# Values before queries in a cross-attention, and two products that walk pass by pass

## The chip, the cores and the metric

The kernel runs on one core of a Trainium2 chip. Its time is the device time of one execution in microseconds (us). Several runs are taken, and their median is the figure that is compared. One further execution is recorded by the hardware profiler, and all views of the profile come from that one.

The engines of a core are called PE (TensorE, matrix products; PEld is its loading of weights), DVE (VectorE), ACT (ScalarE), POOL (GpSimd) and SP (SyncE, which here only issues transfers). Each runs its own queue of instructions in order, and semaphores hold an instruction back until what it needs is there.

## The reference

One layer of a streaming encoder on 512 tokens of width 1024, with 256 memory tokens. What matters here is its middle and the beginning of its last part:

```python
mixed = jnp.sum(gates * proj, axis=2) @ w_out[l]
x = x + _rms_norm(mixed, norm_mix_post[l])

hx = _rms_norm(x, norm_x_pre[l])
m = _rms_norm(mem, norm_mem[l])
xq = (hx @ w_xq[l])                              # 4 heads of 128
xk, xv = jnp.split(m @ w_xkv[l], 2, axis=-1)
sx = einsum('bqhd,bkhd->bhqk', xq, xk) * (X_HEAD_DIM ** -0.5)
px = softmax(sx, axis=-1)
ox = einsum('bhqk,bkhd->bqhd', px, xv).reshape(B, S, X_W) @ w_xo[l]
x = x + _rms_norm(ox, norm_x_post[l])

hf = _rms_norm(x, norm_ffn_pre[l])
u = _dwconv_causal(hf @ w_up[l], ffn_dw[l]) + ffn_dw_b[l]
u_g, u_v = jnp.split(u, 2, axis=-1)
x = x + _rms_norm((silu(u_g) * u_v) @ w_down[l], norm_ffn_post[l])
```

Keys and values (`xk`, `xv`) depend on the memory alone, not on `x`. The queries depend on `hx`, which is only there when the mixers' output projection has been normed.

## The kernel before

**Products in three passes.** All products are kept near fp32 precision by splitting each operand into a high part (fp32r) and a low part (the rest). `mm3` (L185) then issues three matmuls for one product: high weight with high activation, high with low, low with high. The high part of a split is a copy on ACT, the low part a subtraction on DVE (`split`, L106, with its instructions at L109 and L110).

**Weights.** `run_blocks` (L151) draws a list of jobs. A job is one block of weights, 512 KB, and a body that uses it. The block is loaded by SP into one of two raw buffers (`wr`, L123), copied by ACT into one of four high buffers (`wh`, L138), and subtracted by DVE into one of four low buffers (`wl`, L139). Two blocks are fetched ahead. A raw buffer is free for its next load when the low part of the block in it has been made, and a high buffer when the last matmul of the block in it is through.

**The order of the jobs** (`all_jobs`, L1268) is: the mixers, the output projection `mix_out_jobs`, the keys `kx_jobs` (4 blocks), the queries `xq_jobs` (4 blocks), the values `vx_jobs` (4 blocks), the output of the cross-attention `cross_out_jobs` (4 blocks of `w_xo`), the up projection `up_jobs` (44 blocks), the down projection (22 blocks).

- `kx_jobs` (L962) and `xq_jobs` (L1105) use blocks of 128 columns over the full contraction of 1024 (8 pieces of 128). A block gives 24 matmuls of 256 columns, for 256 memory tokens or for half the queries. `xq_jobs` projects the first half of the tokens (tiles 0 and 1) for each head as its block comes, after `drain("n0")`; with the fourth block it drains `"n1"` and projects the second half for all four heads, `part(g, 1)`, out of the four blocks it holds.
- `vx_jobs` (L970) uses blocks of 256 rows of the contraction and all 512 columns. Each gives 12 matmuls of 512 columns, into two PSUM banks that stay open over the four blocks; after the last, both are split into `vxh` and `vxl`.
- `cross_out_jobs` (L1152) holds its four blocks, and then for each half computes `cross_values` (softmax weights times values, into `ox`) and the output product of two tiles.
- `up_jobs` (L1188) computes its first four blocks for the first half of the tokens as the blocks come. With the fourth it drains the last norms and computes the second half of all four (`held`). From the fifth block on the full 512 columns are done at once.

**Work in the background.** `Background` (L44) holds tasks that are written as generators: the softmax of one head and half of the queries (`cross_task`, L1075: scores, exponentials, then transposes into `pth` and `ptl`), and the norm of one tile (`norm_task`, L1000: the residual sum `res`, the squares, the normed tile `nt`, then eight transposes on PE, whose result is split into `hth` and `htl`, the turned activations). A tick lets tasks advance when the foreground has issued enough matmuls; a drain finishes them.

**The final order** on each engine is settled by the framework's scheduler, which moves instructions within what the data allow. The orders of the two built programs can be laid side by side.

**`channel_major`** (L191) is the loop that the change gives a second form of. It goes through the pieces `k` of the contraction and issues the three matmuls of a piece together, so the second matmul already needs the low part of the activations.

Of the kernel before, what the change touches and what calls it, by code (L numbers as in the profile page):

```python
# [25 lines left out]
S = 512  # L26
# [54 lines left out]
def hybrid_layer(ctx: ExitStack, tc: tile.TileContext, a: dict, out: bass.AP):  # L81
# [8 lines left out]
    def bank(tag="mm"):  # L90
        return psum.tile([P, 512], F32, tag=tag, name=f"ps_{tag}", bufs=4 if tag == "mm" else 2)
# [14 lines left out]
    def split(ps, hi, lo, scale=None):  # L106

        if scale is None:
            A.copy(hi, ps)  # L109
            V.tensor_tensor(lo, ps, hi.bitcast(F32), ALU.subtract)  # L110
        else:
            A.activation(hi, ps, AF.Copy if isinstance(scale, float) else AF.Identity, scale=scale)
            V.scalar_tensor_tensor(lo, ps, scale, hi.bitcast(F32), ALU.mult, ALU.subtract)
# [31 lines left out]
    def cols(w, c0, n=P, k0=0, nk=NK):  # L145

        return w[k0 * P:(k0 + nk) * P, c0:c0 + n].rearrange("(k p) c -> p k c", p=P), [P, nk, n]
# [29 lines left out]
    def matmul(ps, lhs, rhs, start, stop):  # L177
        PE.matmul(ps, lhs, rhs, start=start, stop=stop)  # L178
        bg.clock += max(int(math.prod(rhs.shape[1:])), 256) * 0.00042
# [5 lines left out]
    def mm3(ps, w_hi, w_lo, x_hi, x_lo, first, last):  # L185

        matmul(ps, w_hi, x_hi, first, False)
        matmul(ps, w_hi, x_lo, False, False)
        matmul(ps, w_lo, x_hi, False, last)

    def channel_major(ps, w, act, sl=slice(0, S)):  # L191

        hi, lo = w
        nk = hi.shape[1]
        for k in range(nk):
            mm3(ps[:, sl], hi[:, k, :], lo[:, k, :], act[0][:, k, sl], act[1][:, k, sl], k == 0, k == nk - 1)
            if k == 3 < nk - 1:
                bg.tick()

    def rstd_of(pool, parts, n=1):  # L200

        m = pool.tile([P, n], F32, tag="st_m", name="st_m", bufs=4)
        r = pool.tile([P, n], F32, tag="st_r", name="st_r", bufs=4)
        if len(parts) == 2:
            G.tensor_scalar(m, parts[0], parts[1], EPS, ALU.add, ALU.add)  # L205
        else:
            G.tensor_scalar(m, parts[0], EPS, None, ALU.add)
        G.tensor_tensor(r, m, nhalf[:, :n], ALU.pow)  # L208
        return r
# [80 lines left out]
    for i, plan in enumerate(plans):  # L290
        r_t = m1p.tile([P, P], F32, tag="fbias" if i == 2 else "ck", name=f"rows{i}", bufs=2)
        n = 0
# [601 lines left out]
    def then(f):  # L894

        return None, None, f
# [27 lines left out]
    ns = SimpleNamespace()  # L924
# [37 lines left out]
    def kx_jobs():  # L962
        for h in range(4):
            def body(hi, lo, h=h):
                ps = bank()
                channel_major(ps, (hi, lo), ns.mt, slice(0, MEM))
                split(ps[:, :MEM], ns.kx[0][:, h], ns.kx[1][:, h])
            yield *cols(w_xkv, h * P), body

    def vx_jobs():  # L970
        st = {}
        for kb in range(4):
            def body(hi, lo, kb=kb):
                if kb == 0:
                    st["ps"] = [bank() for _ in range(2)]
                for t in range(2):
                    sl = slice(t * P, (t + 1) * P)
                    for k in range(2):
                        kk = kb * 2 + k
                        mm3(st["ps"][t], ns.mt[0][:, kk, sl], ns.mt[1][:, kk, sl], hi[:, k], lo[:, k],  # L980
                            kk == 0, kk == NK - 1)
                    if kb == 3:
                        split(st["ps"][t], ns.vx[0][:, t], ns.vx[1][:, t])
            yield *cols(w_xkv, BR, BR, kb * 2, 2), body
# [90 lines left out]
    def cross_task(h, half):  # L1075

        ps = bank("sc")
        for i in range(2):
            q = slice((2 * half + i) * P, (2 * half + i + 1) * P)
            mm3(ps[:, i * MEM:(i + 1) * MEM], ns.xq[0][:, h, q], ns.xq[1][:, h, q], ns.kx[0][:, h],  # L1080
                ns.kx[1][:, h], True, True)
        p2 = ps.rearrange("p (i k) -> p i k", i=2)
        st = ns.xp.tile([P, 8], F32, tag="st8", name="st8", bufs=4)
        e = ns.xp.tile([P, 2, MEM], F32, tag="xe", name="xe", bufs=5)
        V.tensor_reduce(st[:, 0:2], p2, AX.X, ALU.max)
        V.tensor_scalar(st[:, 2:4], st[:, 0:2], -xscale, None, ALU.mult)
        for i in range(2):
            A.activation(e[:, i], p2[:, i], AF.Exp, bias=st[:, 2 + i:3 + i], scale=xscale,
                         accum_out=st[:, 4 + i:5 + i])
        V.reciprocal(st[:, 6:8], st[:, 4:6])  # L1090
        for i in range(2):
            V.tensor_scalar(e[:, i], e[:, i], st[:, 6 + i:7 + i], None, ALU.mult)
        yield 1.4, 6.0
        while half == 1 and (h, 0) in ns.pt:
            yield 0.0, 0.5
        ps = bank("tr")
        for kt in range(2):
            for i in range(2):
                transpose(ps[:, (2 * kt + i) * P:(2 * kt + i + 1) * P], e[:, i, kt * P:(kt + 1) * P])
        pt = tuple(ns.xp.tile([P, 2, 2 * P], F32R, tag=n, name=n, bufs=4) for n in ("pth", "ptl"))  # L1100
        split(ps.rearrange("p (k c) -> p k c", k=2), pt[0], pt[1])
        ns.pt[h, half] = pt
        yield 0.6, 0.0

    def xq_jobs():  # L1105
        held = []
        for h in range(4):
            def body(hi, lo, h=h):
                held.append((hi, lo))

                def part(h, half):
                    sl = slice(half * 256, (half + 1) * 256)
                    ps = bank()
                    channel_major(ps, held[h], ns.hx, sl)
                    split(ps[:, sl], ns.xq[0][:, h, sl], ns.xq[1][:, h, sl])
                    bg.add(cross_task(h, half), f"x{half}")
                    bg.tick()

                if h == 0:
                    bg.drain("n0")  # L1120
                part(h, 0)
                if h == 3:
                    bg.drain("n1")
                    for g in range(4):
                        part(g, 1)
            yield *cols(w_xq, h * P), body
# [61 lines left out]
    def up_jobs():  # L1188
        st, held = {}, []

        def done(j, i, ps):
            if i == 0:
                st[j] = ns.fp.tile([P, 2, S], F32, tag="c", name="c", bufs=2)
            c, ch = st[j], i * NF + j
            A.activation(c[:, i], ps, AF.Identity, bias=pc("fb", ch), scale=pc("fdw2", ch))  # L1195
            taps(c[:, i], ps, lambda k: pc("fdw01", k * 44 + ch), 3)
            if i == 1:
                th = ns.fp.tile([P, S], F32, tag="th", name="th")
                A.activation(th, c[:, 0], AF.Tanh, scale=0.5)
                V.scalar_tensor_tensor(th, th, 1.0, c[:, 0], ALU.add, ALU.mult)  # L1200
                V.scalar_tensor_tensor(c[:, 1], th, 0.5, c[:, 1], ALU.mult, ALU.mult)  # L1201
                split(c[:, 1], ns.act[0][:, j], ns.act[1][:, j])


        for n in range(2 * NF):
            def body(hi, lo, n=n):
                j, i = divmod(n, 2)
                if n > 3:
                    ps = bank()
                    channel_major(ps, (hi, lo), ns.hf)  # L1210
                    done(j, i, ps)
                    return
                if n == 0:
                    bg.drain("n0")
                ps = bank("mm" if n % 2 else "sc")
                channel_major(ps, (hi, lo), ns.hf, slice(0, S // 2))
                held.append((j, i, ps, (hi, lo)))
                if n == 3:
                    open_ffn()
                    for j, i, ps, w in held:  # L1220
                        channel_major(ps, w, ns.hf, slice(S // 2, S))
                        done(j, i, ps)
            yield *cols(w_up, n % 2 * DFF + n // 2 * P), body

# [43 lines left out]
    def all_jobs():  # L1268
        yield from mixer_jobs()
        yield from last_branch_jobs()  # L1270
        yield then(open_mix_out)
        yield from mix_out_jobs()
        yield then(lambda: bg.drain("mem"))
        yield from kx_jobs()
        yield then(open_cross)
        yield from xq_jobs()
        yield from vx_jobs()
        yield then(open_cross_out)
        yield from cross_out_jobs()
        yield from up_jobs()  # L1280
        yield from down_jobs()

    run_blocks(all_jobs())
    close(ns.fp_)
    close(ns.res_)
# [27 lines left out]
```

## Time and profile before

| | |
|---|---|
| median of 3 runs | 1109.14 us (1108.85 to 1110.48) |
| the profiled execution, its own time | 1108.61 us |
| its span, first to last instruction | 1106.8 us |
| PE busy | 1091.0 us, 99% of the span |
| DVE, ACT, POOL busy | 693.9, 464.9, 97.9 us |
| mean granted clock of PE | 0.998 |

Times in the views are counted from the start of the span. PE's matmuls overlap by a little, so the distance from one start to the next tells its pace better than the length of one. In a view of instructions in order of time, the columns are start and length in us, engine, line, operation, result and inputs by the program's names, size and number; a bracket at the end gives the idle time before it and the instruction that ended the idle time. The keys begin at about 641 us, the queries at 655, the values at about 686, the up projection at 731.

### The profile page before, as it was taken

How to read it: one execution, taken by the hardware profiler on the slowest of the kernel's cores; microseconds unless marked ns; L12 is line 12 of the kernel's file. 1: busy time of each engine (PE TensorE's matmuls, PEld its weight loads, DVE VectorE, ACT ScalarE, POOL GpSimd, SP SyncE). 2: the span in 40 equal slices, each digit the busy share in tenths (PEclk: the TensorE clock that was granted, in tenths of full speed). 3: DMA queues.
4: the chain of work that ended last, by engine and by line, in shares of the span. 5: the costliest groups of instructions: out<-in, count | busy, mean ns of one | idle time of the engine just before them, and what ended most of it. 6: DMA issues, size and time to landing. Idle time of an engine off the chain costs nothing.

```text
span 1106.8 us, 14168 instructions
## 1 busy us (share of the span) xinstructions
PE 1091.0 (99%) x5445; PEld 913.1 (82%) x5445; DVE 693.9 (63%) x1128; ACT 464.9 (42%) x783; POOL 97.9 (9%) x186
## 2 busy tenths in 40 slices
PE   8999999999999999999999999999999999999997
PEld 7888888887878988888888899788888888888886
DVE  5899985457665367857464477677666666642224
ACT  5322222467564255554443365455444444431111
POOL 3000001000101013323010110120000000000001
PEclk9999999999999999999999999999999999999999
DMA  6433432332212243233262253233333333322222
GB/s 197 115 95 94 102 94 81 92 96 58 77 58 78 77 120 104 82 96 107 65 209 96 76 174 115 73 96 115 95 95 95 96 95 95 96 96 95 95 76 76
DMA packets 145849, 109.29 MB, mean 99 GB/s; under 512 B 3648, under 2 KB 133293, under 8 KB 145782
## 3 DMA queue, kind: packets, MB, share of 16 engines
q1 hardware_dynamic: 143221, 99.85, 29.9%
q0 software_dynamic: 2560, 8.54, 2.8%
q8 instruction: 43, 0.70, 0.3%
q14 instruction: 25, 0.20, 0.1%
HBM read 106.27 MB, written 2.11 MB: 98 GB/s over the span
## 4 chain that ended last, share of the span: by engine, by line
PE 94%; DVE 2%; DMA 1%; issue 1%; ACT 1%; POOL 0%; POOLq 0%; DVEq 0%; SPq 0%; ACTq 0%
PE ps_mm L178 80%; PE ps_sc L178 7%; PE ps_tr L182 3%; PE ps_tr L178 3%; PE ps_mm L359 1%; DVE wl L139 1%; DMA wr<-in_w_xo 1%; DMA wr<-in_w_xkv 0%; ACT wh L138 0%; DMA xs<-in_x 0%; POOL st_r L208 0%; DVE e L671 0%; PE ps_tr L343 0%; PE ps_mm L343 0%; ACT hth L109 0%
## 5 line engine op out<-in xcount | busy, mean ns | idle before, releaser
L139 DVE TENSOR_TENSOR wl<-wr,wh 128x1024 fp32r<-128x1024 f32 (+1 forms) x180 | 221.4, 1231 | 221.6 <-ACT wh L138 220.9
L178 PE MATMUL ps_mm<-htl,wh 128*128 128x512 f32 (+1 forms) x944 | 359.9, 381 | 0.0
L178 PE MATMUL ps_mm<-hth,wh 128*128 128x512 f32 (+1 forms) x944 | 359.8, 381 | 0.0
L178 PE MATMUL ps_mm<-hth,wl 128*128 128x512 f32 (+1 forms) x944 | 358.7, 380 | 0.0
L138 ACT CAST wh<-wr 128x1024 fp32r<-128x1024 f32 (+1 forms) x180 | 188.6, 1050 | 349.1 <-PE ps_mm L178 223.0
L178 PEld LDWEIGHTS ps_mm<-hth,wl 128*128 128x128 f32 x944 | 177.4, 188 | 34.5
L178 PEld LDWEIGHTS ps_mm<-hth,wh 128*128 128x128 f32 x944 | 177.6, 188 | 33.9
L178 PEld LDWEIGHTS ps_mm<-htl,wh 128*128 128x128 f32 x944 | 177.6, 188 | 33.0
L507 DVE SCALAR_TENSOR_TENSOR y<-y,par,y 128x499 f32<-128x499 f32 (+28 forms) x120 | 82.7, 729 | 0.2
L178 PE MATMUL ps_mm<-y,wh 128*128 128x512 f32 x256 | 81.2, 395 | 0.0
L441 DVE SCALAR_TENSOR_TENSOR c<-ps_mm,par,c 128x510 f32<-128x510 f32 x84 | 62.6, 746 | 1.4
L178 PEld LDWEIGHTS ps_mm<-y,wh 128*128 128x128 f32 x256 | 47.4, 188 | 10.1
L178 PE MATMUL ps_mm<-y,wl 128*128 128x512 f32 x128 | 50.6, 395 | 0.0
L205 POOL TENSOR_SCALAR st_m<-pm,pm 128x1 f32<-128x1 f32 x12 | 4.6, 387 | 480.6 <-ACT junk L1254 357.0
L109 ACT CAST acth<-c 128x512 fp32r<-128x512 f32 x22 | 13.7, 621 | 55.2 <-DVE c L1201 55.2
L109 ACT CAST pth<-ps_tr 128x512 fp32r<-128x512 f32 (+3 forms) x56 | 23.7, 451 | 27.8 <-PE ps_tr L182 24.9
L178 PE MATMUL ps_mm<-wh,actl 128*128 128x512 f32 x88 | 34.7, 394 | 0.0
L178 PE MATMUL ps_mm<-wl,acth 128*128 128x512 f32 x88 | 34.6, 393 | 0.0
L178 PE MATMUL ps_mm<-wh,acth 128*128 128x512 f32 x88 | 34.4, 394 | 0.0
L110 DVE TENSOR_TENSOR ptl<-ps_tr,pth 128x512 fp32r<-128x512 f32 (+3 forms) x56 | 27.8, 512 | 9.5 <-ACT pth L109 9.1
L1195 ACT ACTIVATE c<-ps_mm,par 128x512 f32<-128x512 f32 x42 | 32.5, 773 | 0.0
L830 POOL TENSOR_SCALAR fbias<-ck,cq 128x128 f32<-128x128 f32 (+3 forms) x32 | 25.5, 805 | 70.6 <-DVE st L836 66.9
(294 smaller groups left out, 1620.3 us busy)
## 6 DMA issues: line engine op xcount, KB each, us to landing
wr<-in_w_up SPq DMA_DIRECT2D x44, 512.0 KB
wr<-in_w_in SPq DMA_DIRECT2D x38, 512.0 KB
wr<-in_w_gate SPq DMA_DIRECT2D x32, 512.0 KB
wr<-in_w_down SPq DMA_DIRECT2D x22, 512.0 KB
wr<-in_w_branch SPq DMA_DIRECT2D x16, 512.0 KB
wr<-in_w_out SPq DMA_DIRECT2D x8, 512.0 KB
wr<-in_w_xkv SPq DMA_DIRECT2D x8, 512.0 KB
wr<-in_w_in SPq DMA_DIRECT2D x4, 520.0 KB
```

The lines of the kernel that those rows point to most:

```text
L109: A.copy(hi, ps)
L110: V.tensor_tensor(lo, ps, hi.bitcast(F32), ALU.subtract)
L138: order(A.copy(hi[:, :n], raw[:, :n]))
L139: low.tensor_tensor(lo[:, :n], raw[:, :n], hi[:, :n].bitcast(F32), ALU.subtract)
L178: PE.matmul(ps, lhs, rhs, start=start, stop=stop)
L182: PE.transpose(ps, x, ident[:n, :n])
L205: G.tensor_scalar(m, parts[0], parts[1], EPS, ALU.add, ALU.add)
L359: keep(PE.matmul(banks[c][:, :S // 2], w[p == 1][:, k, c * P:(c + 1) * P], ht[p == 2][:, i * 4 + k, :S // 2], start=(i, p, k) == (0, 0, 0) ...
L441: V.scalar_tensor_tensor(dst[:, s:], src[:, :S - s], w(k), dst[:, s:], ALU.mult, ALU.add)
L507: V.scalar_tensor_tensor(dst[:, s:], src[:, :S - s], pc("conv_dw", k * 4 + j), dst[:, s:], ALU.mult, ALU.add)
L830: G.tensor_scalar(bias[:, :w], ck[j][:, :w], -1.0, cq[:, qt, head:head + 1], ALU.mult, ALU.add)
L1195: A.activation(c[:, i], ps, AF.Identity, bias=pc("fb", ch), scale=pc("fdw2", ch))
```

## The change

The values are projected directly behind the keys, ahead of the queries. And a new loop, `by_pass`, takes the place of `channel_major` in three places: for head 0 of the queries, in both halves of the tokens, for the first block of the up projection in the first half of the tokens, and for the same block in the second half. It goes over the contraction in two halves of four pieces, and within a half does four matmuls of high with high, four of low weights with high activations, four of high weights with low activations. It does not call `bg.tick()` in the middle, which `channel_major` does. Everything else is as it was.

```diff
+    def by_pass(ps, w, act, sl):
+
+        hi, lo = w
+        nk = hi.shape[1]
+        for h in range(2):
+            ks = range(h * nk // 2, (h + 1) * nk // 2)
+            for i, (w_p, x_p) in enumerate(((hi, act[0]), (lo, act[0]), (hi, act[1]))):
+                for k in ks:
+                    matmul(ps[:, sl], w_p[:, k, :], x_p[:, k, sl], i == k == 0, i == 2 and k == nk - 1)
...
                     ps = bank()
-                    channel_major(ps, held[h], ns.hx, sl)
+                    (channel_major if h else by_pass)(ps, held[h], ns.hx, sl)
...
                 ps = bank("mm" if n % 2 else "sc")
-                channel_major(ps, (hi, lo), ns.hf, slice(0, S // 2))
+                (channel_major if n else by_pass)(ps, (hi, lo), ns.hf, slice(0, S // 2))
...
                     for j, i, ps, w in held:
-                        channel_major(ps, w, ns.hf, slice(S // 2, S))
+                        (channel_major if i or j else by_pass)(ps, w, ns.hf, slice(S // 2, S))
                         done(j, i, ps)
...
         yield from kx_jobs()
+        yield from vx_jobs()
         yield then(open_cross)
         yield from xq_jobs()
-        yield from vx_jobs()
         yield then(open_cross_out)
         yield from cross_out_jobs()
```

## Prediction

> **What bounds the kernel now.** I read the page first: the busy times, the chain that ended last, the granted clock. TensorE (PE) is busy for 99% of the span, holds 94% of the chain, and runs at its full clock in all 40 slices.
>
> ```profile
> PE 1091.0 (99%) x5445; PEld 913.1 (82%) x5445; DVE 693.9 (63%) x1128; ACT 464.9 (42%) x783; POOL 97.9 (9%) x186
> ...
> PEclk9999999999999999999999999999999999999999
> ...
> PE 94%; DVE 2%; DMA 1%; issue 1%; ACT 1%; POOL 0%; POOLq 0%; DVEq 0%; SPq 0%; ACTq 0%
> ```
>
> The change removes no matmul, so it can act only through moments in which PE stands still. The instruction orders of the two built programs say where to look: they agree on every engine up to the first query product (655.33 in the profile before) and again from the fifth up-projection block (about 755). The table by stretches and the list of what PE waited for cover that stretch and the one ahead of it.
>
> ```profile
> 640.00:655.00 15.00, 14.26 (x117) 13.80 (x116) 14.19 (x17) 8.48 (x15) 3.54 (x8) 1.00 0.58 176
> 685.00:700.00 15.00, 14.54 (x78) 12.22 (x76) 9.11 (x15) 7.33 (x12) 0.00 (x0) 1.00 0.49 167
> 700.00:710.00 10.00, 8.90 (x47) 7.21 (x48) 5.75 (x15) 4.36 (x13) 0.00 (x0) 1.00 0.18 54
> 730.00:740.00 10.00, 9.67 (x75) 8.99 (x74) 9.11 (x11) 6.17 (x12) 3.19 (x4) 1.00 0.50 144
> 740.00:750.00 10.00, 9.76 (x82) 9.33 (x81) 3.17 (x4) 1.49 (x3) 1.35 (x3) 1.00 0.21 71
> ...
> PE ps_mm L178 <- DVE vxl L110: 0.8, 1, 0.8
> PE ps_tr L182 <- DVE xe L1092: 0.7, 1, 0.7
> PE ps_mm L178 <- ACT wh L138: 0.7, 1, 0.7
> PE ps_sc L178 <- ACT hth L109: 0.2, 1, 0.2
> PE ps_sc L178 <- DVE htl L110: 0.2, 1, 0.2
> ```
>
> First number behind the comma: PE's busy time in the stretch. The 0.7 us behind `wh` lies in the keys (640 to 655) and stays. The others add to two pieces: the end of the values (`vxl`, `xe`, near 700) and the start of the up projection (`htl`, `hth`, near 732 and 745). So at most some 3 us of 1108.61 are to be had.
>
> **What goes: the wait at the values.** Today the values are the last thing projected before they are used, and the last half of the queries' softmax has just begun. These are the starts of PE's instructions there.
>
> ```profile
> 699.26 0.28 PE L178 MATMUL ps_mm<-ptl,vxh 128*128 128x256 f32 x1
> 700.35 0.38 PE L178 MATMUL ps_mm<-pth,vxl 128*128 128x256 f32 x1 [0.81 <-DVE vxl L110]
> ...
> 702.00 0.28 PE L178 MATMUL ps_mm<-pth,vxl 128*128 128x256 f32 x1
> 703.02 0.72 PE L182 MATMUL ps_tr<-ident,xe 128*128 128x128 f32 x4 [0.74 <-DVE xe L1092]
> 703.73 0.50 PE L178 MATMUL ps_mm<-wh,oxh 128*128 128x512 f32 x1
> ...
> 569.50 48.85 PE ps_mm L178 x211
> 557.26 0.87 PE ps_tr L182 x8
> 655.37 4.65 PE ps_mm L178 x39
> ```
>
> The last three rows, from the chain in order of time, give PE's undisturbed pace: 48.85/211 = 0.232 us for a 512-column matmul, 4.65/39 = 0.119 for a 256-column one, 0.109 for a transpose. Against them the starts lose 1.09 - 0.12 = 0.97, 1.02 - 0.12 = 0.90 and 0.71 - 0.44 = 0.27 us: **2.1 us**. In the new order `vx` is done before the first query product, and the softmax of the first half runs beside the 96 matmuls (11.4 us) of the queries' second half, so these waits go. What is late next: with no values in between, the first softmax transposes of the second half stand behind two further score blocks and among the output products; I find cover for each.
>
> **What goes: the start of the up projection.** Here PE waits for the transposed second tile, high part (ACT) and low part (DVE).
>
> ```profile
> 731.43 0.28 PE L178 MATMUL ps_mm<-hth,wh 128*128 128x256 f32 x1
> 731.85 0.39 PE L178 MATMUL ps_sc<-hth,wh 128*128 128x256 f32 x1
> 732.44 0.38 PE L178 MATMUL ps_sc<-htl,wh 128*128 128x256 f32 x1 [0.20 <-DVE htl L110]
> ...
> 746.01 0.28 PE L178 MATMUL ps_mm<-hth,wh 128*128 128x256 f32 x1
> 746.27 0.39 PE L178 MATMUL ps_sc<-htl,wh 128*128 128x256 f32 x1
> ```
>
> Lost over 0.12 per step: 0.30 + 0.47 = 0.77 us, and 0.14 in the second half. By passes, eight matmuls that need only the high part (4 of `wh`, 4 of `wl`, 0.95 us) stand ahead of the first that needs `htl`. That covers 0.47 and 0.14. The 0.30 is a wait of block 2's first product, which the built order moves behind block 1. Gone: **0.9 us**. `by_pass` itself issues the same 24 matmuls per block at the same pace: no cost. At the queries it removes nothing, since nothing waits there today.
>
> **What comes: twelve weight blocks in a row.** The values' 4 blocks (12 matmuls of 512 columns, 2.78 us each) now stand between the keys' 4 and the first-half queries' 4 (24 of 256, 2.86 us). SP's load of block n+2 waits until DVE has made the low part of block n (two raw buffers), so a buffer's cycle is landing + cast + low part against 5.6 us of PE. Today the queries' second halves, which need no weights, part the eight from the next eight. The four loads of values move past the four of queries on SP's queue; POOL's order is unchanged.
>
> ```profile
> 653.32 1.22 DVE L139 TENSOR_TENSOR wl<-wr,wh 128x1024 fp32r<-128x1024 f32 x1
> 653.70 0.59 POOL L1149 DMA_DIRECT2D g_pre<-in_norm_ffn_pre  x1 [1.62 <-DVE nt L218]
> 660.32 1.05 ACT L138 CAST wh<-wr 128x1024 fp32r<-128x1024 f32 x1 [1.31 <-DMA wr<-in_w_xq]
> 661.40 1.23 DVE L139 TENSOR_TENSOR wl<-wr,wh 128x1024 fp32r<-128x1024 f32 x1 [1.94 <-ACT wh L138]
> ...
> 751.54 1.23 DVE L139 TENSOR_TENSOR wl<-wr,wh 128x1024 fp32r<-128x1024 f32 x1 [4.73 <-ACT wh L138]
> 753.35 1.22 DVE L139 TENSOR_TENSOR wl<-wr,wh 128x1024 fp32r<-128x1024 f32 x1
> 756.37 1.05 ACT L138 CAST wh<-wr 128x1024 fp32r<-128x1024 f32 x1 [0.42 <-DMA wr<-in_w_up]
> 758.75 1.05 ACT L138 CAST wh<-wr 128x1024 fp32r<-128x1024 f32 x1 [0.65 <-DMA wr<-in_w_up]
> ...
> 693.21 3.49 DMA wr<-in_w_xo
> ```
>
> Let L be the time from the end of a low part to the start of the next cast in that buffer. Undisturbed: 756.37 - 752.77 = 3.60 and 758.75 - 754.57 = 4.18 (w_up, laid out like w_xq); beside POOL's gain load (653.70): 660.32 - 654.54 = 5.78. Nothing but weights is in flight when the queries now load, so I take L = 3.9, nearest the w_up rows. Cast and low part take 1.05 + 1.23 = 2.28.
>
> PE reaches the third value block at 655.33 + 24 x 0.232 + 0.87 (eight transposes) = 661.8 and after two matmuls (662.2) needs its low part. That block has the place the third query block has today, ready at 661.40 + 1.23 = 662.63: a stall of 0 to 0.4, say 0.2. From 662.63 the 22 matmuls left of the values (5.1) and, by passes, four of query block 0 (0.5) last to 668.2; its low part is ready at 662.63 + L + 2.28: a stall of L - 3.3. Then 20 + 24 + 4 matmuls (5.7 us) to the low part of query block 2: a stall of L + 2.28 - 5.7 = L - 3.4. Sum 2L - 6.5: **1.3 us** at L = 3.9; 0.5 to 2.1 over L = 3.60 to 4.18. ACT's cast of query block 2 now waits for a load with the high part of head 0's queries queued behind it, for which PE's scores wait; the 0.37 us of that cast ends before the low part (1.23) that PE needs next, so it adds nothing.
>
> The Trainium skill, *DMA: Bandwidth & Descriptors*, section on the anatomy of one DMA (gpsimd path), gives a fixed 2.0 us plus bytes over 436 GB/s, which by estimate is 3.2 us for 512 KB and would make 2L - 6.5 about zero. These rows show 3.49 to 5.78 on SP's queue, so the trace does not agree, and the rows decide.
>
> **A smaller new wait.** After the first output tile, PE needs it normed. Today that chain runs from `junk` to `nt`:
>
> ```profile
> 711.94 0.60 ACT L996 ACTIVATE junk<-ps_mm 128x512 f32<-128x512 f32 x1 [0.19 <-PE ps_mm L178]
> 717.95 1.28 DVE L218 SCALAR_TENSOR_TENSOR nt<-res,st_r,g_pre 128x1024 f32<-128x1024 f32 x1
> ```
>
> That is 719.23 - 711.94 = 7.3 us, 7.5 with the idle 0.19. The new order puts 18 matmuls of 512 columns, 19 of 256 and 10 transposes over it, 4.2 + 2.2 + 1.1 = 7.5: no margin. I take 0.25, bounds 0 and 0.6.
>
> **Sum.** -2.1 - 0.9 + 1.3 + 0.25 = -1.5 us (bounds -2.5 and -0.3). The profiled execution took 1108.61 (span 1106.8 and 1.8 around it), so 1107.1; the median of the runs, 1109.14, lies 0.5 higher: **1107.6**. About 0.2%, 2.2 us, is what a measurement of this kernel can tell from no change, so the likeliest reading is "the same", a little below.
>
> **Rivals.**
> - *The loads don't keep up* (slower). If the queries' loads land as late as today's beside POOL's, L = 5.78 in both cycles, the feed costs 5.1 and the sum is +2.3: 1111.4. It turns slower than before at 2L - 6.5 = 2.75, L = 4.6, and by over 0.2% at L = 5.7. For it: today's load of the third query block shows that L. Against: the gain load is over by then.
> - *The loads keep up.* With L at 3.49, as the chain shows for w_xo, and the values (laid out like w_xo) landing earlier, the feed costs 0.2: -2.6, 1106.5. The Trainium skill's formula above points here too.
> - *The wait only moves.* The second half's softmax now hangs on PE's own late scores; if 2.1 us return as waits on `xe` or `pth`, -1.5 becomes +0.6: 1109.7. Against: 8 us of output products lie between the last scores and their transposes, and the chain from scores to `xe` has five short steps.
> - *Less than said.* That `by_pass` does nothing at the queries I already count.
>
> **Chances.** Forecast 0.58, loads keep up 0.17, the wait moves 0.13, loads don't keep up 0.12. Faster by over 0.2% (below 1106.9): most of the second case and a quarter of the first, 0.30. Slower by over 0.2% (above 1111.4): 0.10. Between: 0.60. The forecast's own range is 1106.6 to 1108.9; with the second and third case and 0.4 of measurement, 1105.8 to 1110.8, which leaves out most of the last.
>
> **What would show it.** After: no wait on `vxl` and none on `xe` of 0.5 or more; PE's waits between 660 and 677 are on `wh` and `wl` from w_xkv and w_xq, two or three of them, 1.3 us together; the up projection starts without the 0.77; everything beyond about 755 only shifted. Waits on `wl` of 2 us or more, or a sum of waits unchanged with other names, would make it wrong.

## The result and the profile after

The changed kernel takes 1107.42 us (median of 20 runs, 1104.78 to 1109.07) against 1109.44 us (median of 20 runs, 1107.63 to 1111.64) for the kernel before: a ratio of 0.9981, 95% interval 0.9974 to 0.9987, which is 2.1 us less (1.4 to 2.9). The forecast was 1107.6. The execution that was profiled took 1107.43 us, at the median; the one of before, 1108.61, lies 0.8 under its median, so the two traces show a smaller difference than the runs.

From the page after: the busy times and shares, and the chain by engine and by line.

```profile
PE 1089.8 (99%) x5445; PEld 912.3 (83%) x5445; DVE 694.9 (63%) x1128; ACT 465.3 (42%) x783; POOL 98.7 (9%) x186
...
PE 94%; DMA 2%; DVE 2%; ACT 1%; issue 0%; POOL 0%; POOLq 0%; DVEq 0%; SPq 0%; ACTq 0%
PE ps_mm L178 80%; PE ps_sc L178 7%; PE ps_tr L182 3%; PE ps_tr L178 3%; PE ps_mm L369 1%; DVE wl L139 1%; DMA wr<-in_w_xkv 1%; DMA wr<-in_w_xq 1%; ACT wh L138 0%; DMA xs<-in_x 0%; DVE e L681 0%; POOL st_r L218 0%; PE ps_tr L353 0%; ACT nt L224 0%; ACT hth L109 0%
```

The by-engine shares are nearly as before, with DMA at 2% for 1%. In the row by line the loads of `w_xkv` and `w_xq` now have 1% each; before, `w_xkv` had 0%, `w_xo` 1%, and `w_xq` did not appear in the row. The low parts `wl` had 1% before too. The list of what PE waited for between 600 and 800 us says it directly (columns: total us, times, longest):

```profile
PE ps_mm L178 <- DVE wl L139: 1.5, 3, 0.5
PE ps_mm L178 <- ACT wh L138: 1.0, 2, 0.8
PE ps_sc L178 <- ACT hth L109: 0.2, 1, 0.2
```

The names `vxl`, `xe` and `htl` are gone; `wl` has come, three times. (0.8 of the 1.0 on `wh` is the keys' wait, there before too.) The table by stretches, PE's busy time first behind the comma:

```profile
655.00:670.00 15.00, 13.77 (x67) 10.82 (x66) 8.10 (x10) 7.11 (x12) 0.00 (x0) 1.00 0.55 168
670.00:685.00 15.00, 14.51 (x122) 14.22 (x122) 9.58 (x21) 6.38 (x16) 0.00 (x0) 1.00 0.45 141
685.00:700.00 15.00, 15.00 (x131) 15.00 (x130) 11.83 (x26) 9.58 (x24) 0.00 (x0) 1.00 0.33 106
700.00:710.00 10.00, 10.00 (x59) 8.66 (x59) 6.84 (x20) 5.05 (x17) 0.00 (x0) 1.00 0.19 55
730.00:740.00 10.00, 10.00 (x82) 9.69 (x81) 9.32 (x11) 6.17 (x11) 3.76 (x5) 1.00 0.51 146
```

685 to 700, 700 to 710 and 730 to 740 are full now (14.54, 8.90 and 9.67 before); 655 to 685 shows PE idle for 1.7 us. The starts of PE's instructions there, where a 512-column matmul takes 0.232 us and a 256-column one 0.119:

```profile
661.05 0.70 PE L178 MATMUL ps_mm<-wh,mth 128*128 128x512 f32 x2
662.28 0.50 PE L178 MATMUL ps_mm<-wl,mth 128*128 128x512 f32 x1 [0.52 <-DVE wl L139]
...
667.26 0.40 PE L178 MATMUL ps_mm<-wh,mtl 128*128 128x512 f32 x1
667.85 0.74 PE L178 MATMUL ps_mm<-hth,wh 128*128 128x256 f32 x4 [0.19 <-ACT wh L138]
669.11 0.74 PE L178 MATMUL ps_mm<-hth,wl 128*128 128x256 f32 x4 [0.52 <-DVE wl L139]
...
674.76 0.28 PE L178 MATMUL ps_sc<-kxl,xqh 128*128 128x256 f32 x1
675.53 0.38 PE L178 MATMUL ps_mm<-hth,wl 128*128 128x256 f32 x1 [0.49 <-DVE wl L139]
```

Lost: 1.23 - 2 x 0.232 = 0.77 at the third value block, 0.59 - 0.23 = 0.36 and 1.26 - 0.47 = 0.79 at query block 0, 0.77 - 0.12 = 0.65 at query block 2. Together **2.6 us**, where the prediction had 1.3. The weights' side, and POOL's load of the gain:

```profile
652.80 1.22 DVE L139 TENSOR_TENSOR wl<-wr,wh 128x1024 fp32r<-128x1024 f32 x1
653.18 0.59 POOL L1159 DMA_DIRECT2D g_pre<-in_norm_ffn_pre  x1 [1.62 <-DVE nt L228]
...
659.92 1.05 ACT L138 CAST wh<-wr 128x1024 fp32r<-128x1024 f32 x1 [3.46 <-DMA wr<-in_w_xkv]
661.00 2.55 DVE L139 TENSOR_TENSOR wl<-wr,wh 128x1024 fp32r<-128x1024 f32 x2 [3.00 <-ACT wh L138]
666.75 1.05 ACT L138 CAST wh<-wr 128x1024 fp32r<-128x1024 f32 x1 [3.49 <-DMA wr<-in_w_xq]
667.83 1.22 DVE L139 TENSOR_TENSOR wl<-wr,wh 128x1024 fp32r<-128x1024 f32 x1 [3.08 <-ACT wh L138]
673.17 1.05 ACT L138 CAST wh<-wr 128x1024 fp32r<-128x1024 f32 x1 [2.69 <-DMA wr<-in_w_xq]
...
g_pre<-in_norm_ffn_pre POOLq DMA_DIRECT2D x1, 512.0 KB, 5.4
```

The last row is from the list of DMA issues: 512 KB, 5.4 us from issue to landing, so the gain's load is in flight from 653.2 to 658.6.

With L as the prediction defined it (end of a low part to the start of the next cast in that buffer): 659.92 - 654.02 = 5.90 for the third value block, 666.75 - 662.23 = 4.5 for query block 0 (the row at 661.00 holds two low parts of 1.23, and the first of them ends then), 673.17 - 669.05 = 4.12 for query block 2.

### The profile page after: what moved, and what is told of

It reads as the page before. It is cut to its first block, busy times and chain, and to the rows that moved or that the text cites. A ratio compares the mean times of both kernels' runs of the same rounds, so it can differ in the third digit from the quotient of the medians.

```text
span 1105.6 us, 14172 instructions
## 1 busy us (share of the span) xinstructions
PE 1089.8 (99%) x5445; PEld 912.3 (83%) x5445; DVE 694.9 (63%) x1128; ACT 465.3 (42%) x783; POOL 98.7 (9%) x186
## 4 chain that ended last, share of the span: by engine, by line
PE 94%; DMA 2%; DVE 2%; ACT 1%; issue 0%; POOL 0%; POOLq 0%; DVEq 0%; SPq 0%; ACTq 0%
PE ps_mm L178 80%; PE ps_sc L178 7%; PE ps_tr L182 3%; PE ps_tr L178 3%; PE ps_mm L369 1%; DVE wl L139 1%; DMA wr<-in_w_xkv 1%; DMA wr<-in_w_xq 1%; ACT wh L138 0%; DMA xs<-in_x 0%; DVE e L681 0%; POOL st_r L218 0%; PE ps_tr L353 0%; ACT nt L224 0%; ACT hth L109 0%
## 5 line engine op out<-in xcount | busy, mean ns | idle before, releaser
L1209 ACT ACTIVATE th<-c 128x512 f32<-128x512 f32 x22 | 13.9, 631 | 41.2 <-DVE c L451 41.2
```

## What PE lost, kernel by kernel

All kernels do the same work between the first key product (641.25 before, 640.65 after) and the first 512-column product of the up projection (757.08 and 755.87), up to small shifts of order. "Stretch" is the time between these two starts, and the other columns are what PE's starts lose in it, read as above, everything over 0.12: in the keys; on weight blocks from the values on and on the queries' own low parts and exponentials ("feed and queries"); from the use of the values to the output products ("exit"); and at the start of the up projection. The wait on the up projection's second half (`hth`, 0.40 in each) is left out of the columns. Stretch and losses come from one profiled execution, the ratio from the runs.

| kernel | keys | feed and queries | exit | start of up | stretch | ratio to before (95%) |
|---|---|---|---|---|---|---|
| before | 0.89 | 0 | 2.15 | 0.91 | 115.83 | 1 |
| after | 0.98 | 2.57 | 0 | 0 | 115.22 | 0.9981 (0.9974 to 0.9987) |
| after, again | 0.81 | 1.20 | 0 | 0 | 113.54 | 0.9977 (0.9967 to 0.9987) |
| move alone | 0.79 | 1.35 | 0.71 | 0.16 | 115.01 | 0.9983 (0.9975 to 0.9992) |
| loop alone | 0.85 | 0 | 1.83 | 0 | 114.49 | 0.9991 (0.9982 to 1.0000) |
| after, loop at queries only | 0.85 | 1.02 | 0 | 1.02 | 114.54 | 0.9989 (0.9980 to 0.9998) |
| after, third raw buffer | 0.25 | 0 | 0 | 0 | 111.49 | 0.9965 (0.9952 to 0.9977) |
| after, gain early | 0.36 | 0.69 | 0 | 0 | 112.54 | 0.9967 (0.9955 to 0.9980) |
| the same again | 0.80 | 0.23 | 0 | 0 | 112.50 | 0.9964 (0.9951 to 0.9976) |
| after, two heads whole | 0.76 | 0.94 | 1.59 | 0 | 115.57 | 0.9996 (0.9987 to 1.0005) |
| before, third raw buffer | 0.77 | 0 | 2.08 | 0.90 | 115.61 | 0.9997 (0.9988 to 1.0006) |
| before, gain early | 0.44 | 0.66 | 2.09 | 0.91 | 116.17 | 0.9997 (0.9988 to 1.0006) |

What is left of the stretch without these losses and the 0.40 lies between 110.8 and 111.9 us in all twelve. The stretches themselves lie up to 4.7 us apart, so the losses read off the starts account for most of the differences, but not for the last half microsecond or so of any one of them.

## The experiments

### The parts alone, and the change once more

The move alone keeps `channel_major` everywhere (this cut is against the changed kernel):

```diff
-                    (channel_major if h else by_pass)(ps, held[h], ns.hx, sl)
+                    channel_major(ps, held[h], ns.hx, sl)
```

(and the same at the two places of the up projection).

> Only the values are moved in front of the queries; every product keeps the three matmuls of a piece together. Theory A (waits of PE taken away, a slower feed of weights added, and nothing else): the 2.1 us at the values go, the feed of twelve blocks costs the 1.3 to 2.6 us that forecast and profile after name, the 0.8 us at the start of the up projection stay or change by at most 0.3. So -0.8 to +0.5 us against before, and PE's waits near the values' end gone, those on wl and wh between 660 and 677 as in the profile after. Rival B (the move alone brings all of the 2 us, the pass order nothing): -2.0 us. Rival C (the move brings nothing or harm, all comes from the pass order): 0 or slower, with waits on vxl or xe back.

1107.37 us against 1108.92, ratio 0.9983 (0.9975 to 0.9992), which is 1.9 us less (0.9 to 2.8): better than theory A's -0.8 to +0.5, and about what rival B said. By its time the move alone can't be told from the whole change; only the traces, and the kernel with the loop at the queries only further down, part the two. The values' waits go, the feed takes 1.35 back, and one new wait stands among the output products. From PE's starts:

```profile
716.08 0.28 PE L178 MATMUL ps_mm<-pth,vxh 128*128 128x256 f32 x1
716.91 0.51 PE L178 MATMUL ps_mm<-wh,oxh 128*128 128x512 f32 x1 [0.56 <-ACT oxh L109]
...
728.21 0.60 PE L182 MATMUL ps_tr<-ident,nt 128*128 128x128 f32 x4
...
731.22 0.28 PE L178 MATMUL ps_sc<-hth,wh 128*128 128x256 f32 x1
```

The 0.83 between the first two is a wait on the high part of the cross-attention's output, 0.71 us lost. The last two rows were not expected: the up projection starts without a wait although it still walks piece by piece. In this built order the second tile's last transposes stand at 728.21, with eleven output products behind them before the first up product (a later expectation counts twelve); in the kernel before it is six.

The loop alone leaves the values where they were (against the changed kernel):

```diff
         yield from kx_jobs()
-        yield from vx_jobs()
         yield then(open_cross)
         yield from xq_jobs()
+        yield from vx_jobs()
```

> Only the pass order, in its three places; the values stay behind the queries. Theory A: -0.6 to -0.9 us, all of it at the start of the up projection (no wait on htl there), while the waits on vxl and xe near 700 stay as before and the queries are no faster. Rival B: 0. Rival C: -2.0 us.

1108.14 us, ratio 0.9991 (0.9982 to 1.0000), at the edge of no change. What PE waited for, 600 to 800 us:

```profile
PE ps_tr L182 <- DVE xe L1102: 0.7, 1, 0.7
...
PE ps_mm L178 <- DVE vxl L110: 0.5, 1, 0.5
...
```

`htl` is gone, and with it the 0.91 at the start of the up projection; `vxl` and `xe` are not. At the queries the loop changes nothing, as there was nothing to remove.

The change once more is the same kernel.

> The changed kernel once more, for a second profile beside the others on one chip. Theory A: -1.4 to -2.9 us against before, as in the first twenty runs; the feed's waits of the first profile (2.6 us) come again if they belong to the order, and vary by 0.5 us or more if they hang on how late single loads land. A rival: the first profile's waits were an accident and the feed costs under 1 us here.

1106.26 us, ratio 0.9977. The same waits, with other sizes:

```profile
PE ps_mm L178 <- ACT wh L138: 0.7, 1, 0.7
PE ps_mm L178 <- DVE wl L139: 0.6, 2, 0.4
...
```

The feed costs 0.24, 0.41 and 0.55 here, 1.20 in all. Four executions have this order of blocks with nothing done about the loads (after, its repeat, the move alone, and the loop at the queries only): the third value block's L is 5.90, 5.41, 5.18 and 5.03 in them, and the feed costs 2.57, 1.20, 1.35 and 1.02. PE stalls at that block itself only in the first two. The execution recorded first is the dearest of the four.

### A third raw buffer, after and before

The third value block and the second query block are loaded into a tile that is free at that time, so that these two loads need not wait for a low part, and those behind them can start a block earlier:

```diff
+        raw = spare() if spare else gp.tile([P, WB], F32, tag="wr", name="wr", bufs=2)
...
+            yield *cols(w_xkv, BR, BR, kb * 2, 2), body, *third(kb == 2)
...
+            yield *cols(w_xq, h * P), body, *third(h == 1)
```

> The changed kernel with a third raw buffer for this stretch: the third block of the values and the second of the queries are loaded into a tile that the memory's norm has left free, so that every load from there on can go out one block earlier. Theory A (the feed's waits come from the cycle landing + cast + low part of two raw buffers): the waits on wh and wl between 660 and 677 fall from 2.6 to under 1 us, and the time by 1.6 to 2.6 us against the changed kernel. Rival D (the transfers themselves are the limit: three 512 KB loads in flight share the same engines, so each lands later): waits fall by under 0.8 us, and the time from the end of a low part to the landing grows by more than 1 us.

1104.81 us, ratio 0.9965. Of the waits between 600 and 800 us one is left:

```profile
PE ps_sc L178 <- ACT hth L109: 0.2, 1, 0.2
```

So the feed is a matter of when the loads may start. This kernel is about 4 us faster than the one before; some 0.6 of that lies at the keys, whose wait is 0.25 here. Against the changed kernel's two ratios (0.9981 and 0.9977) it is 1.3 to 1.8 us less, at the lower end of what was expected. The control puts the same buffer into the kernel before.

> The kernel before, with a third raw buffer in the same two places as in the changed kernel with a third raw buffer (the third value block and the second query block). Theory (PE lost nothing to the feed before the change, since the queries' second halves part the blocks): the waits on vxl (0.97 us of PE's starts) and xe (0.90 and 0.27) and those at the start of the up projection stay, and the time is the same within 0.5 us, ratio 1.000. Rival (the third buffer is a gain of its own, with or without the change): 1.0 us or more faster, ratio 0.999 or less.

Ratio 0.9997 (0.9988 to 1.0006): nothing that can be measured. Its waits from 600 to 800 us:

```profile
PE ps_mm L178 <- DVE vxl L110: 0.7, 1, 0.7
PE ps_tr L182 <- DVE xe L1095: 0.7, 1, 0.7
...
```

They are those of before. The third buffer is no gain of its own: it frees what the change had lost.

### One load of POOL out of the way

The gain of the feed-forward norm, loaded by POOL at 653 us, is loaded ahead of the keys into another tile. The third value block's L was the longest of all, and this transfer is what ran beside it.

```diff
-        ns.post, ns.pre = stage("s0", "g_post2"), stage("s1", "g_pre2")
+        ns.post, ns.pre = stage("s0", "g_post2"), ns.pre2
...
-        G.dma_start(ns.pre, a["norm_ffn_pre"][0].partition_broadcast(P))
...
+    def open_keys():
+        bg.drain("mem")
+        ns.pre2 = stage("s2", "g_pre2")
+        G.dma_start(ns.pre2, a["norm_ffn_pre"][0].partition_broadcast(P))
...
-        yield then(lambda: bg.drain("mem"))
+        yield then(open_keys)
```

> The changed kernel, with one load moved: the gain of the feed-forward norm (512 KB, issued by POOL at 653 us, between the low parts that release the loads of the third and fourth value blocks) is loaded some 15 us earlier, right when the keys begin. Theory (POOL's load shares the transfer with the weights and stretches the third value block's time L, 5.90 us in the changed kernel, 5.41 in its repeat): L of the third value block falls to about 4.5, and PE's stall in front of that block's low part (0.77 and 0.24 us in the two executions) is gone; 0.2 to 0.8 us faster than the changed kernel, ratio to before about 0.997. Rival (the two weight blocks in flight share one queue and are late by themselves): L stays over 5.2 and the stall stays; ratio as the changed kernel's, 0.998. The keys' wait of 0.8 us may grow, since the load now runs beside theirs: up to +0.5.

1105.16 us against 1109.24, ratio 0.9967. The scheduler issued the load at 569.59 us, much earlier than expected. The rows of the one raw buffer, to be laid beside those of after:

```profile
652.91 1.22 DVE L139 TENSOR_TENSOR wl<-wr,wh 128x1024 fp32r<-128x1024 f32 x1 [0.26 <-ACT wh L138]
657.79 1.05 ACT L138 CAST wh<-wr 128x1024 fp32r<-128x1024 f32 x1 [1.16 <-DMA wr<-in_w_xkv]
658.88 1.23 DVE L139 TENSOR_TENSOR wl<-wr,wh 128x1024 fp32r<-128x1024 f32 x1 [0.70 <-ACT wh L138]
664.07 1.05 ACT L138 CAST wh<-wr 128x1024 fp32r<-128x1024 f32 x1 [1.57 <-DMA wr<-in_w_xq]
665.15 1.23 DVE L139 TENSOR_TENSOR wl<-wr,wh 128x1024 fp32r<-128x1024 f32 x1 [1.17 <-ACT wh L138]
670.20 1.05 ACT L138 CAST wh<-wr 128x1024 fp32r<-128x1024 f32 x1 [1.14 <-DMA wr<-in_w_xq]
```

And what PE waited for from 600 to 800 us:

```profile
PE ps_sc L178 <- DVE xql L110: 0.5, 1, 0.5
...
PE ps_mm L178 <- ACT wh L138: 0.2, 1, 0.2
```

L is 657.79 - 654.13 = 3.66, 664.07 - 660.11 = 3.96 and 670.20 - 666.38 = 3.82 (the other buffer's three: 3.83, 4.26, 4.13). PE waits for no weight block between 655 and 680; the 0.2 on `wh` is the keys'. The 0.53 on the queries' own low part (`xql`) is new. So the theory held, and by more than it had said: not only the third value block's stall is gone but those of the queries' blocks behind it. At query block 2 it is close: its low part ends at 672.51 and is used at 672.56. Up to that product PE issues what it issues in the changed kernel, in the same order but for two scores and two products that change places, so PE's order explains none of it. The kernel was then run and recorded once more.

> The changed kernel with the early gain load, once more. Theory (POOL's load starts the delay and the ring of two raw buffers hands it on to the queries' blocks): L is between 3.6 and 4.3 us for all six blocks from the third value block on, PE waits on no block of w_xkv's values and none of w_xq (0.2 us together at most; 1.0 to 2.6 us in the four executions with the load at its place), ratio 0.997. Rival (the feed varies by itself from execution to execution, and one was lucky): 1 us or more of stalls on wh and wl between 660 and 677 us returns, ratio 0.998.

1105.45 us against 1109.75, ratio 0.9964. L is 3.70 to 4.19 for all six blocks. The waits of 600 to 800 us are:

```profile
PE ps_mm L178 <- ACT wh L138: 0.6, 1, 0.6
...
```

Again the 0.6 is the keys'. Against the changed kernel's two ratios those of the early gain (0.9967 and 0.9964) are 1.1 to 1.9 us lower. The intervals of the single ratios touch, so this rests on the traces as well: 2.57 and 1.20 us lost on weight blocks there, none here. The control is the kernel before with the same load moved.

> The kernel before, with the same one load moved: the gain of the feed-forward norm is loaded ahead of the keys (it was issued at 570 us in the changed kernel with the early load) and not at 653 us. Theory (the load costs time only where weight blocks stand in a row; before the change the queries' second halves, 11.4 us, give the late block its time, and PE lost nothing there): the third query block's L falls from 5.78 to about 4 us, but the waits on vxl, xe and at the start of the up projection stay, and the time is the same within 0.5 us, ratio 1.000. Rival (the early load is a gain of its own in either order): 1.0 us or more faster, ratio 0.999 or less.

Ratio 0.9997 (0.9988 to 1.0006). The third query block's L falls to 658.61 - 654.51 = 4.10 (5.78 before), and nothing comes of it:

```profile
PE ps_mm L178 <- DVE vxl L110: 0.9, 1, 0.9
...
PE ps_tr L182 <- DVE xe L1092: 0.7, 1, 0.7
...
```

The waits at the values stand as before. (The 0.66 in its row of the table is a wait for the first query block, which no other kernel shows.)

### Spreading the blocks instead

The queries' heads 0 and 1 project both halves of the tokens as their block comes. Not shown in the cut: the buffers of the softmax weights grow from 4 to 6, and those of the exponentials (`xe`) shrink from 5 to 4.

```diff
                 part(h, 0)
+                if h < 2:
+                    bg.drain("n1")
+                    part(h, 1)
                 if h == 3:
-                    bg.drain("n1")
-                    for g in range(4):
+                    for g in range(2, 4):
```

> The changed kernel, but heads 0 and 1 of the queries project both halves of the tokens when their block comes (48 matmuls of 256 columns, 5.7 us a block instead of 2.86), heads 2 and 3 as before; the buffers of the softmax weights grow from 4 to 6 and those of the exponentials shrink from 5 to 4. Theory (the feed stalls because twelve blocks stand in a row at 2.8 us each, against a buffer's cycle of 6.2 to 8 us for two): the stall at the third query block (0.65 and 0.55 us) is gone, those at the third value block and query block 0 stay, and with the exit unharmed the time is 0.5 us under the changed kernel's, ratio 0.9975. Rival: the softmax of the first half is put later by the earlier second halves and the exit waits again for its transposes, 0.5 to 1.5 us, ratio 0.999.

1109.02 us, ratio 0.9996 (0.9987 to 1.0005): the rival. (The recorded execution took 1111.29, but its keys begin at 644.18, 2.9 later than in before, so that excess lies ahead of the stretch.) The feed's stalls are gone, at all three places; at the third value block they are absent in the move alone too. But PE waits for the queries' low part and the exponentials (0.94 us lost) and then at the exit (1.59):

```profile
...
PE ps_sc L178 <- DVE xql L110: 0.3, 1, 0.3
PE ps_mm L178 <- DVE ptl L110: 0.3, 1, 0.3
PE ps_sc L178 <- ACT xe L1098: 0.3, 1, 0.3
...
```

Here "the wait only moves", the third rival of the prediction, is what happens. A likely reason is that the second halves were the cover of the first half's softmax; as the buffers of the exponentials were changed along with them, this is not shown.

### The loop at the queries only

```diff
-                (channel_major if n else by_pass)(ps, (hi, lo), ns.hf, slice(0, S // 2))
+                channel_major(ps, (hi, lo), ns.hf, slice(0, S // 2))
```

(and in the second half of the up projection).

> The changed kernel with the pass-by-pass loop at the queries alone; the up projection walks piece by piece again. In the built order seven output products stand between the last transposes and the first up product, as in the changed kernel (six in the kernel before, twelve with the move alone). Theory (the loop covers what the place of the transposes does not): PE loses 0.3 to 0.55 us at the start of the up projection and 0.15 in its second half, which the loop had covered; 0.5 to 0.7 us slower than the changed kernel, ratio to before 0.9985. Rival (after the move the start of the up projection needs no cover, as in the kernel with the move alone): no loss at the start, 0.15 in the second half, ratio as the changed kernel's.

1108.21 us, ratio 0.9989 (0.9980 to 0.9998). PE's starts at the up projection:

```profile
731.33 0.28 PE L178 MATMUL ps_mm<-hth,wh 128*128 128x256 f32 x1
732.33 0.39 PE L178 MATMUL ps_sc<-htl,wh 128*128 128x256 f32 x1 [0.72 <-DVE htl L110]
```

1.00 - 0.12 = 0.88 lost, more than the 0.3 to 0.55 expected, and 0.14 in the second half: the theory. In the changed kernel the loop has eight matmuls ahead of the first low part there, and no loss:

```profile
731.11 0.64 PE L178 MATMUL ps_sc<-hth,wh 128*128 128x256 f32 x4
731.59 0.64 PE L178 MATMUL ps_sc<-hth,wl 128*128 128x256 f32 x4
...
732.23 0.74 PE L178 MATMUL ps_sc<-htl,wh 128*128 128x256 f32 x4
```

So in this built order the loop is worth 1.0 us at the up projection. With the move alone another built order gave the cover for nothing; the two parts of the change overlap there.

## Why the prediction came out right, and which step was wrong

**The sum** said -1.5; the runs say -2.1 (1.4 to 2.9), the repeat -2.6 (1.4 to 3.7). The forecast of 1107.6 holds. That it is only 0.2 off is partly luck: it was added to a median of 1109.14 from three runs, and the same -1.5 from the 1109.44 of twenty would have been 1107.9. Between the two traces the stretch is only 0.6 us shorter, because the recorded execution of after had the dearest feed; the repeat's is 2.3 shorter.

**The values' exit, -2.1:** right. The 2.15 us of before are gone after and in the repeat, and no wait on `xe` or `pth` took their place.

**The start of the up projection, -0.9:** right in size, and the covers named were there. That the move alone would remove the 0.77 as well, by another place for the transposes, was not foreseen.

**The feed, +1.3 (0.5 to 2.1):** the size holds in three of four executions; the recorded one has 2.57, at four waits on `wl` and `wh` where two or three were forecast. The step behind it fails. The prediction took twelve blocks in a row as the cause and wrote the cost as 2L - 6.5 with L of the queries' loads. With the gain's load out of the way L is 3.66 to 4.26, around the 3.9 it had taken, the twelve blocks still stand in a row, and they cost nothing. Nor is the late block enough by itself: before, it stands there with its L of 5.78, and PE loses nothing to the feed. It takes both. The constant 6.5 hid this: it starts from the third value block ready at 662.63, a time read from before, which already held the delay beside the gain's load. Without it that block is ready 5.78 - 3.9 = 1.9 earlier, at 660.7; query block 0's low part then is at 660.7 + 3.9 + 2.28 = 666.9, 0.9 ahead of PE's need at 667.8, and query block 2's at 673.1, 0.4 ahead of 673.5: no stall. The two executions show none, at query block 2 by less than 0.1. The prediction named 0.2 for the delay, at its own block, and carried the rest unseen inside the 6.5. The block that is late releases its raw buffer late, so the next block in that buffer starts late, and the next again: the queries' blocks paid most of it. In the recorded execution query block 0's own L was 4.5 on top, over the bound of 4.18; what stretched it is open. "The gain load is over by then" was true of the transfer and not of its delay.

**The new wait at the first normed tile, +0.25 (0 to 0.6):** it did not come.

```profile
710.35 0.60 ACT L1006 ACTIVATE junk<-ps_mm 128x512 f32<-128x512 f32 x1 [0.18 <-PE ps_mm L178]
...
715.73 1.29 DVE L228 SCALAR_TENSOR_TENSOR nt<-res,st_r,g_pre 128x1024 f32<-128x1024 f32 x1 [0.98 <-POOL st_r L218]
...
717.66 0.60 PE L182 MATMUL ps_tr<-ident,nt 128*128 128x128 f32 x4
```

The normed tile is there at 717.02, and its first transpose stands at 717.66 without a wait. PE's work over the chain is the 7.5 us that were counted (from 710.17, where `junk`'s input is ready). The chain was the mis-sized term: from `junk` to `nt` it takes 717.02 - 710.35 = 6.7 us here, not the 7.3 read from before.

**`by_pass` at the queries, nothing:** true by itself (the loop alone). Behind the move it puts four matmuls and not two ahead of query block 0's low part. The losses there, 1.12 with the piece-by-piece loop against 1.15, 0.41 and 0.38 with the other, do not settle what that is worth. What these four do follow is that block's own L: 4.39 and 4.52 with the two large losses, 3.80 and 3.87 with the two small.

**The rivals.** "Loads don't keep up" had the right L and place for one block, not for both cycles. "Loads keep up" is what the early gain makes true: 1105.2 and 1105.5 us, 1 us below that rival's 1106.5. The third value block no longer stalls (0.2 in the prediction) and the wait at the first normed tile is nothing (0.25), which explains about half of this; the rest stays open. The formula of the Trainium skill that the prediction named for this rival (*DMA: Bandwidth & Descriptors*, anatomy of one DMA) is given for the gpsimd path, and the rows held against it are SP's, so they neither confirm nor refute it. Both that kernel and the one with the third raw buffer beat the two kernels compared here.

## What to carry to other kernels

When a change puts blocks of weights closer together, ask first what else is in flight there: one foreign transfer of 512 KB delayed one block, the two-buffer ring handed that on to the blocks behind it, and moving that single load was worth 1 to 2 us on top of a change that brought 2. A constant in an estimate that is read from the old trace carries that trace's disturbances; take it apart before it is used. And a wait that two parts of a change each remove is to be counted once.

## What the runs showed of the chip

For SP's loads of 512 KB, L (from the free buffer to the cast) is 3.66 to 4.26 us with weights alone in flight (twelve cases in two executions); with POOL's 512 KB beside it, 5.03 to 5.90 for the first and 3.80 to 4.77 for the second of the two blocks (four executions). The Trainium skill, *DMA: Bandwidth & Descriptors*, section on queues, rings and completion order, says that a DMA engine takes turns between the queues it has work for, packet by packet. At the 436 GB/s of that page (its section on the anatomy of one DMA, gpsimd path) 512 KB more would be 1.2 us by estimate; the first block was 1.3 to 2.2 us later than the 3.66 and 3.70 of the two undisturbed executions, so the rule agrees in direction, and the bytes alone explain the lower end of it.

The same program's stalls on its weights differ by more than a microsecond from one execution to the next (2.57 and 1.20 us), with the same instructions in the same order, so one recorded execution doesn't size a term of 1 or 2 us.
